# A hybrid attention layer on one core: k and q interleaved by channel in DRAM, and a later product with the softmax reciprocals

## The chip, the cores and the metric

The kernel runs on one core of one Trainium2 chip. The time is the device time of one execution in microseconds; lower is better. A core has five engines that run their own instruction streams and wait for each other by semaphores: TensorE (PE, with its weight loads PEld), VectorE (DVE), ScalarE (ACT), GpSimd (POOL) and SyncE (SP). Here SP computes nothing: it issues nearly all the DMA transfers, one after the other. POOL issues a few.

## The reference

One post-norm residual layer on x of 512 positions by 2048 channels, all in float32. One projection by w_in gives eight blocks of 1024 columns: q, k, v and a gate for each of two head groups, 16 heads of 64 channels each.

```python
h = einsum(x, w_in); qa, ka, va, ga, qb, kb, vb, gb = split(h)
# group A: three dilated windows, merged with weights proportional to their denominators, T5 bias
ya = dilated_attention(qa, ka, va, t5_bias)
# group B: windows of 8 rows x 16 columns on the 8 x 64 grid of positions, learned 2-D bias
yb = neighbourhood_attention(qb, kb, vb, na_rpb)
y  = concat(ya * silu(ga), yb * silu(gb))
x  = layer_norm(alpha * x + y @ w_out)
```

Everything goes through softmax(q k / 8 + bias) v per head, with masks that differ by group.

## The kernel before

**Numbers in two parts.** Float32 operands of TensorE are split into a high part (rounded to the matmul type) and a low part (the rest). A product takes three matmuls: high x high, high x low, low x high. ScalarE makes the high part (a copy), VectorE the low part (a subtraction). In the names, `wh` and `wl` are the two parts of weights, `th` and `tl` of the turned probabilities, `yk` of the gated output.

**Stages.** First the projections: a plain block of gate columns, then the blocks k, q, v of group 0, k of group 1, a block of gates, q and v of group 1, each a seven-product Strassen scheme (`strassen_block`, run by `run_blocks`). A block of 28 jobs loads its weights in 16 tiles of 512 KB (`braw`). Their results are turned, split and stored to DRAM by `store_kq` and `store_v`. Then attention: 16 pairs of heads, groups in turn, each head in four query blocks, so 128 steps of scores and some more for what follows them. Into its steps filler matmuls are mixed (`fill`): the remaining gate units and half of the output projection. Then the other half of the output projection and the layer norm.

**The q and k tiles.** `store_kq` holds for two heads of a pair a tile `kst`: 128 partitions (64 channels of head a = 0, then of a = 1), high and low. A k tile goes to `k_d[pair]` as [high/low, channel, head, position]; in SBUF the load puts high rows on partitions 0 to 63 and low rows on 64 to 127. A q tile goes to `q_d[pair]` as [high/low, 128 rows of head and channel, position], in rows of 64 positions (256 bytes). `load_kq` reads for a pair one k tile and three q tiles: high on both halves of `qt`, low on the lower half of `ql`. The upper half of `ql` is zeroed once for each of two buffers. Scores are then two matmuls: `qt` with k (high x high + high x low), `ql` with k (low x high).

**Steps of attention.** Step n works on pair i = n // 8. In it stand the scores of block n, the reduction on VectorE that adds the bias and takes the minimum (L623, `s` and `mn`), the exponential on ScalarE (L627, `p`), and the turning of the probabilities of step n - 2 on TensorE (`pt`, L686) with their split (L691, L692). At steps with n % 4 = 2 TensorE multiplies the turned probabilities of a head by v (`pv`, L708); the two halves are added on ScalarE (L832) and VectorE (L833) into `y`. `pv` takes one of the two "sc" buffers in PSUM that the scores use.

**Normalisation.** A pair's eight denominators are inverted at n % 8 = 0 (L844), turned at n % 8 = 1 by `share`, sent to DRAM and read back broadcast into `rc` by POOL (L722, L724). `gate` multiplies `y` by the gate at n % 8 = 4 (L731). `gated` then queues three operations: y times rc on VectorE (L739), the high part on ScalarE a step later (L740), the low part on VectorE two steps later (L741). Here `gated` of pair i - 1 is called at n % 8 = 7 of pair i.

**What sets the order.** On PE, DVE and ACT the projections and attention stand as the program is written (a manual schedule); in attention SP's order is written too. During the projections SP's and POOL's orders come from a scheduler that works on a timeline of its own. `later(k, ...)` puts an operation at the end of the k-th step from now; an operation for VectorE that falls on a step with n % 4 = 1 is held until after the next step's reduction.

Of the kernel before, what the change touches and what calls it, by code (L numbers as in the profile page):

```python
# [6 lines left out]
F32 = mybir.dt.float32  # L7
# [6 lines left out]
S = 512  # L14
H = 16
KT = D // 128
PAIRS = 8
# [42 lines left out]
def _view(t, offset, dims):  # L60
    return bass.AP(tensor=t.tensor, offset=t.offset + offset, ap=dims)
# [10 lines left out]
def hybrid_layer(tc, xT, xn, w_in, w_early, w_mid, w_gate, w_out, t5x, brow, rpb, cmask, eye, gain, lbias, out):  # L72
    nc = tc.nc
    from contextlib import ExitStack
    with ExitStack() as ctx:
# [8 lines left out]
        def f(ap):  # L84
            return ap.bitcast(F32)
# [44 lines left out]

        rows_d = dram.tile([H, 16, ROW], F32, name="rows_d")
        bias_d = dram.tile([H, 128, 560], F32, name="biasa_d"), dram.tile([H, 128, BW], F32, name="biasb_d")
        k_d = [dram.tile([PAIRS, 2, 64, 2, S], F32, name=f"k{g}_d") for g in range(2)]
        q_d = [dram.tile([PAIRS, 2, 128, S], F32, name=f"q{g}_d") for g in range(2)]
        sg_d = dram.tile([2 * PAIRS, 128, S], F32, name="sg_d")
        rc_d = dram.tile([2 * PAIRS, 8, 128], F32, name="rc_d")
        v_d = [dram.tile([PAIRS, 128, 4, 256], F32, name=f"v{g}_d") for g in range(2)]
# [92 lines left out]
        def store_kq(kind, g, ch, half, b, src):  # L230

            o = vst.next("kst", F32R)
            hi, lo = o[:, 0:512], o[:, 512:1024]
            if kind == "k":
                split(src, hi, lo)
            else:
                nc.scalar.activation(hi, src, AF.Copy, scale=-0.125)
                nc.vector.scalar_tensor_tensor(lo, src, -0.125, f(hi), op0=ALU.mult, op1=ALU.subtract)
            o = o.rearrange("p (s n q) -> p s n q", s=2, n=2)
            for n in range(2):  # L240
                for i in range(2):
                    if kind == "k":
                        to = k_d[g][4 * ch + 2 * b + n].rearrange("s c a q -> c s a q")[:, :, i]
                        nc.sync.dma_start(to[:, :, HALF * half:HALF * half + HALF], f(o[64 * i:64 * i + 64, :, n]))
                    else:
                        to = q_d[g][4 * ch + 2 * b + n][i].rearrange("c (b h q) -> c h b q", b=4, h=2)[:, half]
                        nc.sync.dma_start(to, f(o[:, i, n].rearrange("p (b q) -> p b q", b=4)))

        def turned_out(kind, two, b):

# [323 lines left out]
        lows = []  # L574
        for i in range(2):
            ql = slot(f"t{4 * i + 3}", F32R, "ql").rearrange("p (a n) -> p a n", a=2)
            nc.gpsimd.memset(f(ql[64:128]), 0.0)
            lows.append(ql)

        def load_kq(i):  # L580

            g, j = ORDER[i]
            t0 = 4 * (i % 2)
            kt = slot(f"t{t0}", F32R, "k").rearrange("p (a n) -> p a n", a=2)
            qt = slot(f"t{t0 + 1}", F32R, "q").rearrange("p (a n) -> p a n", a=2)
            ql = lows[i % 2]

            nc.sync.dma_start(f(kt.rearrange("p a n -> p (a n)")), k_d[g][j].rearrange("s c a q -> (s c) (a q)"))
            for n, to in enumerate((qt[0:64], qt[64:128], ql[0:64])):
                nc.sync.dma_start(f(to), q_d[g][j][n // 2].rearrange("(a c) q -> c a q", a=2))  # L590
            loaded[i] = qt, ql, kt

        def load_v(i):
# [212 lines left out]
        with tc.manual_schedule(engines=engines):  # L806
# [6 lines left out]
            for n in range(136):  # L813
                b, i = n % 4, n // 8
                mixing = n % 4 == 2 and 6 <= n <= 130
                amount = ((8, 6, 1, 6) if n < 64 else (8, 7, 1, 7))[b]
                if b == 0 and n < 124:
                    load_bias(n // 4 + 1)
                if n % 8 == 0 and n < 120:
                    load_kq(i + 1)  # L820
                if n % 8 == 4 and n < 128:
                    if n < 120:
                        load_v(i + 1)
                    load_sg(i)
                exponent = scores(n) if n < 128 else None
                while held:
                    held.pop(0)()
                if mixing:
                    if exponent:
                        exponent()  # L830
                    mine, theirs, y, t = values(n // 4 - 1)
                    nc.scalar.activation(t, theirs, AF.Copy)  # L832
                    nc.vector.tensor_tensor(y, mine, t, ALU.add)  # L833
                    fill(amount)
                else:
                    fill(amount // 2)
                if 2 <= n < 130:
                    turn(n - 2)
                if not mixing:
                    if exponent:  # L840
                        exponent()
                    fill(amount - amount // 2)
                if n >= 8 and n % 8 == 0:
                    later(0, lambda i=i: nc.vector.reciprocal(dens[i - 1], dens[i - 1]), True)  # L844
                if n >= 8 and n % 8 == 1:
                    share(i - 1)
                if n >= 8 and n % 8 == 4:
                    later(0, lambda i=i: gate(i - 1), True)
                if n >= 8 and n % 8 == 7:
                    gated(i - 1)  # L850
                close()
            while tasks:
# [144 lines left out]
        for dc in (2, 3):  # L997
            for u in range(4, 8):
                raw = out_ring.next("wraw")
                nc.sync.dma_start(raw[:, :1024], w_out[8 * dc + u])  # L1000
                i = 2 * (u - 4)
# [92 lines left out]
```

## Time and profile before

| | |
|---|---|
| median of 3 runs | 974.61 us (974.07 to 975.96) |
| profiled execution | 975.21 us, span 973.4 us |
| granted TensorE clock | 0.999 |
| TensorE busy | 964.3 us (99%) |
| VectorE, ScalarE, POOL busy | 757.0, 496.3, 181.3 us |
| read from and written to HBM | 148.69 and 44.50 MB |

The span runs from the first to the last instruction. A row of instructions gives the engine, the line of the program, the operation, what it writes and reads, a count and the busy time; in brackets or behind a bar stands the idle time of that engine before it, and the instruction that ended it. In a timeline the first two numbers are the start and the length in microseconds, of several instructions where a count follows. "SPq" rows are issues: what they move lands later. A tile is named without its buffer's number.

### The profile page before, as it was taken

Reading aid. Unit: us, or ns where it says so; the run is one execution under the profiler, and the core shown is the slowest. Engines: PE = TensorE matmul, PEld = TensorE weight load, DVE = VectorE, ACT = ScalarE, POOL = GpSimd, SP = SyncE. Lnnn points to the kernel's source line nnn. Section 1 sums busy time; section 2 is a strip of 40 time slices with the busy share of each in tenths; the row PEclk is TensorE's granted clock in tenths of the full one; section 3 lists DMA queues with packets and bytes.
Section 4 is the critical chain, followed back from the end, with each engine's and each line's share of the span. In section 5 each row is a group of like instructions: output and inputs, shape, how many; then the busy total and the mean of one; then the engine's idle time right before and its main releaser. Section 6 shows DMA issues by size and latency. Waiting matters only on the chain. (4 is left out here: it accounts for less than half of the span.)

```text
span 973.4 us, 13993 instructions
## 1 busy us (share of the span) xinstructions
PE 964.3 (99%) x4789; PEld 803.6 (83%) x4789; DVE 757.0 (78%) x1144; ACT 496.3 (51%) x857; POOL 181.3 (19%) x323
## 2 busy tenths in 40 slices
PE   8999999999999999999999999999999999999997
PEld 6887888888888889988888888888888888888886
DVE  7897778679789777796788856777776777777877
ACT  7454444444444344443445446776766766672300
POOL 1006656835636000000000000011111000100020
PEclk9999999999999999999999999999999999999999
DMA  9715796698396087420872687887887678779213
GB/s 336 277 65 133 229 329 210 171 296 235 107 350 207 33 282 206 163 93 17 266 182 103 206 271 209 224 234 212 236 239 218 204 228 204 209 219 314 91 58 117
DMA packets 120263, 194.18 MB, mean 199 GB/s; under 512 B 49455, under 2 KB 69807, under 8 KB 120192
## 3 DMA queue, kind: packets, MB, share of 16 engines
q1 hardware_dynamic: 107520, 169.68, 57.3%
q0 software_dynamic: 12096, 22.95, 8.5%
q8 instruction: 38, 0.62, 0.3%
q10 hardware_dynamic: 576, 0.66, 0.2%
q14 instruction: 33, 0.27, 0.1%
HBM read 148.69 MB, written 44.50 MB: 198 GB/s over the span
## 5 line engine op out<-in xcount | busy, mean ns | idle before, releaser
L376 ACT ACTIVATE wh<-braw 128x1024 fp32r<-128x1024 f32 x182 | 193.3, 1062 | 269.2 <-PE acc L404 206.5
L381 DVE TENSOR_TENSOR wl<-braw,wh 128x1024 fp32r<-128x1024 f32 x182 | 223.6, 1230 | 53.8 <-ACT wh L376 53.6
L403 PE MATMUL acc<-wh,xk 128*128 128x512 f32 x384 | 151.3, 394 | 0.0
L405 PE MATMUL acc<-wl,xk 128*128 128x512 f32 x384 | 149.7, 390 | 0.0
L404 PE MATMUL acc<-wh,xk 128*128 128x512 f32 x384 | 149.5, 389 | 0.0
L372 DVE TENSOR_TENSOR braw<-braw 128x1024 f32<-128x1024 f32 x104 | 126.6, 1217 | 0.1
L403 PE MATMUL acc<-wh,op 128*128 128x512 f32 x288 | 113.1, 393 | 0.0
L405 PE MATMUL acc<-wl,op 128*128 128x512 f32 x288 | 112.2, 390 | 0.0
L404 PE MATMUL acc<-wh,op 128*128 128x512 f32 x288 | 112.1, 389 | 0.0
L756 PE MATMUL acc<-wh,yk 128*128 128x512 f32 x320 | 108.1, 401 | 0.0
L692 DVE TENSOR_TENSOR tl<-pt,th 128x256 fp32r<-128x256 f32 (+1 forms) x128 | 71.0, 555 | 35.8 <-ACT th L691 34.1
L691 ACT ACTIVATE th<-pt 128x256 fp32r<-128x256 f32 (+1 forms) x128 | 62.3, 489 | 47.6 <-PE pt L686 45.4
L403 PEld LDWEIGHTS acc<-wh,xk 128*128 128x128 f32 x384 | 72.1, 188 | 15.3 <-ACT bias L151 0.9
L405 PEld LDWEIGHTS acc<-wl,xk 128*128 128x128 f32 x384 | 72.1, 188 | 15.2
L404 PEld LDWEIGHTS acc<-wh,xk 128*128 128x128 f32 x384 | 72.2, 188 | 14.5
L627 ACT ACTIVATE p<-s,mn 128x512 f32<-128x512 f32 (+1 forms) x96 | 62.2, 648 | 29.4 <-DVE mn L623 29.0
L623 DVE CUSTOM_DVE_ANT_0 s<-sc,biases 128x512 f32<-128x512 f32 (+2 forms) x128 | 67.7, 529 | 10.8 <-PE sc L667 10.0
L562 PE MATMUL acc<-xk,wh 128*128 128x512 f32 x256 | 75.3, 404 | 0.0
L756 PEld LDWEIGHTS acc<-wh,yk 128*128 128x128 f32 x320 | 58.5, 189 | 8.8
L161 POOL DMA_DIRECT2D bias<-rows_d x128 | 61.6, 489 | 17.6 <-DMA biasa_d<-bias 5.5
L756 PE MATMUL acc<-wl,yk 128*128 128x512 f32 x160 | 63.9, 403 | 0.0
L405 PEld LDWEIGHTS acc<-wl,op 128*128 128x128 f32 x288 | 54.1, 188 | 11.4
(188 smaller groups left out, 1708.2 us busy)
## 6 DMA issues: line engine op xcount, KB each, us to landing
braw<-in_w_in SPq DMA_DIRECT2D x96, 512.0 KB
wraw<-in_w_out SPq DMA_DIRECT2D x32, 512.0 KB
k_d<-kst SPq DMA_DIRECT2D x64, 128.0 KB
q_d<-kst SPq DMA_DIRECT2D x64, 128.0 KB
v_d<-vst SPq DMA_DIRECT2D x32, 256.0 KB
q<-q_d SPq DMA_DIRECT2D x32, 256.0 KB
wraw<-in_w_gate SPq DMA_DIRECT2D x16, 512.0 KB
k<-k_d SPq DMA_DIRECT2D x16, 512.0 KB
```

The source lines that it names most:

```text
L372: nc.vector.tensor_tensor(raws[q][u], raws[q][u], raws[other][u], ALU.add)
L376: nc.scalar.activation(h, raws[q][u], AF.Copy)
L381: nc.vector.tensor_tensor(l, raws[q][u], f(h), ALU.subtract)
L403: nc.tensor.matmul(accs[t], ah[:, q], h[:, c], start=first and k == 0, stop=False, skip_group_check=skip)
L404: nc.tensor.matmul(accs[t], al[:, q], h[:, c], start=False, stop=False, skip_group_check=skip)
L405: nc.tensor.matmul(accs[t], ah[:, q], l[:, c], start=False, stop=k == 7, skip_group_check=skip)
L562: nc.tensor.matmul(acc, w[:, k * 128:k * 128 + 128], X[8 * u + k][:, s], start=u == 0 and n == 0 and k == 0, stop=u == 1 and n == 2 and k ...
L623: nc.vector.tensor_tensor_reduce(*flat, bias, 1.0, 3e38, ALU.add, ALU.min, mn)
L627: nc.scalar.activation(p[:, to:to + n].rearrange("p (b r c) -> p b r c", r=8, c=c), s[:, :n].rearrange(order, r=8, c=c), AF.Exp, bias=mn, ...
L691: nc.scalar.activation(th, pt[:, :nch], AF.Copy)
L692: nc.vector.tensor_tensor(tl, pt[:, :nch], f(th), ALU.subtract)
L756: nc.tensor.matmul(acc[:, part], yk[k][:, s, c], w[:, wk], start=first and kk == 0 and n == 0, stop=last and kk == 1 and n == 2)
```

## The change

The k tile is stored and loaded as [channel, high/low, head, position], so that partition 2c holds the high row of channel c and 2c + 1 its low row. The q tile is stored as [high/low, channel, head, position]; a channel's two heads now stand side by side, so a row to load has 4096 bytes. Since the two heads lie on different partitions of `kst`, a store of q is cut in two, one a head. `qt` is loaded by one transfer that reads each row twice (a step of 0), `ql` by one that fills the even partitions; the odd ones are zero, and the zeroing covers the whole tile. `gated(i - 2)` is called at n % 8 = 1 for pairs 0 to 13; the last two pairs keep their steps.

```diff
-        k_d = [dram.tile([PAIRS, 2, 64, 2, S], F32, name=f"k{g}_d") for g in range(2)]
-        q_d = [dram.tile([PAIRS, 2, 128, S], F32, name=f"q{g}_d") for g in range(2)]
+        k_d = [dram.tile([PAIRS, 64, 2, 2, S], F32, name=f"k{g}_d") for g in range(2)]
+        q_d = [dram.tile([PAIRS, 2, 64, 2, S], F32, name=f"q{g}_d") for g in range(2)]
...
-                        to = k_d[g][4 * ch + 2 * b + n].rearrange("s c a q -> c s a q")[:, :, i]
+                        to = k_d[g][4 * ch + 2 * b + n][:, :, i]
                         nc.sync.dma_start(to[:, :, HALF * half:HALF * half + HALF], f(o[64 * i:64 * i + 64, :, n]))
                     else:
-                        to = q_d[g][4 * ch + 2 * b + n][i].rearrange("c (b h q) -> c h b q", b=4, h=2)[:, half]
-                        nc.sync.dma_start(to, f(o[:, i, n].rearrange("p (b q) -> p b q", b=4)))
+                        to = q_d[g][4 * ch + 2 * b + n][i].rearrange("c a (b h q) -> c a h b q", b=4, h=2)[:, :, half]
+                        for a in range(2):
+                            nc.sync.dma_start(to[:, a], f(o[64 * a:64 * a + 64, i, n].rearrange("p (b q) -> p b q", b=4)))
...
-            nc.gpsimd.memset(f(ql[64:128]), 0.0)
+            nc.gpsimd.memset(f(ql), 0.0)
...
-            nc.sync.dma_start(f(kt.rearrange("p a n -> p (a n)")), k_d[g][j].rearrange("s c a q -> (s c) (a q)"))
-            for n, to in enumerate((qt[0:64], qt[64:128], ql[0:64])):
-                nc.sync.dma_start(f(to), q_d[g][j][n // 2].rearrange("(a c) q -> c a q", a=2))
+            nc.sync.dma_start(f(kt.rearrange("p a n -> p (a n)")), k_d[g][j].rearrange("c s a q -> (c s) (a q)"))
+            nc.sync.dma_start(f(qt.rearrange("p a n -> p (a n)")), _view(q_d[g], j * 256 * S, [[2 * S, 64], [0, 2], [1, 2 * S]]))
+            nc.sync.dma_start(f(ql[0:128:2].rearrange("p a n -> p (a n)")), q_d[g][j][1].rearrange("c a q -> c (a q)"))
...
-                if n >= 8 and n % 8 == 7:
+                if n % 8 == 1 and 2 <= i < 2 * PAIRS:
+                    gated(i - 2)
+                if n % 8 == 7 and i >= 2 * PAIRS - 1:
                     gated(i - 1)
```

TensorE's order is the same. SP, from the stores of group 1's q to the end of the loads of x that follow (`q_d` the stores, `braw` the weights of the next block, `xback` the part of x that attention's fillers need again), before:

```order
L247 DMA q_d<-kst 512x1x64 x4
L360 DMA braw<-in_w_in 128x1024
L247 DMA q_d<-kst 512x1x64 x4
L360 DMA braw<-in_w_in 128x1024 x7
L247 DMA q_d<-kst 512x1x64 x4
L360 DMA braw<-in_w_in 128x1024
L247 DMA q_d<-kst 512x1x64 x4
L360 DMA braw<-in_w_in 128x1024
L247 DMA q_d<-kst 512x1x64 x16
L522 DMA xback<-in_xT 128x256 x5
L360 DMA braw<-in_w_in 128x1024
L522 DMA xback<-in_xT 128x256 x3
```

and now:

```order
L248 DMA q_d<-kst 64x4x64 x16
L361 DMA braw<-in_w_in 128x1024 x2
L248 DMA q_d<-kst 64x4x64 x8
L361 DMA braw<-in_w_in 128x1024 x4
L248 DMA q_d<-kst 64x4x64 x8
L361 DMA braw<-in_w_in 128x1024 x4
L248 DMA q_d<-kst 64x4x64 x32
L361 DMA braw<-in_w_in 128x1024 x3
L523 DMA xback<-in_xT 128x256
L361 DMA braw<-in_w_in 128x1024
L523 DMA xback<-in_xT 128x256 x7
```

There are 64 stores for 32, the weight loads stand behind more of them, and seven of the eight loads of x have moved behind four weight loads. On VectorE the splits of that x (`xk<-xback`) have moved with them, in the new order:

```order
L373 TENSOR_TENSOR braw<-braw 128x1024
L89 TENSOR_TENSOR xk_98<-xback,xk_98 128x256
L382 TENSOR_TENSOR wl<-braw,wh 128x1024
L89 TENSOR_TENSOR xk_99<-xback,xk_99 128x256
L89 TENSOR_TENSOR xk_100<-xback,xk_100 128x256
L89 TENSOR_TENSOR xk_101<-xback,xk_101 128x256
L89 TENSOR_TENSOR xk_102<-xback,xk_102 128x256
L89 TENSOR_TENSOR xk_103<-xback,xk_103 128x256
L89 TENSOR_TENSOR xk_104<-xback,xk_104 128x256
L382 TENSOR_TENSOR wl<-braw,wh 128x1024
L89 TENSOR_TENSOR xk_105<-xback,xk_105 128x256
L382 TENSOR_TENSOR wl<-braw,wh 128x1024 x2
```

Before, they stood one or two at a time between the `wl` and `braw` operations of five earlier jobs; now six stand in one piece. In attention, VectorE of pair 2 from step 18 to step 21 (`ISA` is the reduction of the scores, `y<-y,rc` the product with the reciprocals, `yk` the low part), before:

```order
L741 SCALAR_TENSOR_TENSOR yk<-y,yk 128x512
L833 TENSOR_TENSOR y<-pv,tmp 64x512
L692 TENSOR_TENSOR tl<-pt,th 128x4x128
L568 SCALAR_TENSOR_TENSOR sgo<-sgo,acc 128x512
L623 ISA s,mn<-sc,biases 128x512
L623 ISA mn 128x1
L692 TENSOR_TENSOR tl<-pt,th 128x4x128
L548 TENSOR_TENSOR wl<-wraw,wh 128x1024
L623 ISA s,mn<-sc,biases 128x512
L623 ISA mn 128x1
L692 TENSOR_TENSOR tl<-pt,th 128x4x128
L731 TENSOR_TENSOR y<-y,sg 128x512
```

and now:

```order
L740 TENSOR_TENSOR y<-y,rc 128x512
L834 TENSOR_TENSOR y<-pv,tmp 64x512
L693 TENSOR_TENSOR tl<-pt,th 128x4x128
L569 SCALAR_TENSOR_TENSOR sgo<-sgo,acc 128x512
L624 ISA s,mn<-sc,biases 128x512
L624 ISA mn 128x1
L693 TENSOR_TENSOR tl<-pt,th 128x4x128
L549 TENSOR_TENSOR wl<-wraw,wh 128x1024
L742 SCALAR_TENSOR_TENSOR yk<-y,yk 128x512
L624 ISA s,mn<-sc,biases 128x512
L624 ISA mn 128x1
L693 TENSOR_TENSOR tl<-pt,th 128x4x128
```

The product has taken the low part's place at step 18, and the low part stands at the end of step 19, behind `wl`. At step 15, where the product stood behind another `wl`, nothing has come in its stead.

## The prediction

> **What bounds the kernel now.** I read the page's first two parts first, then the busy time by stage, then what the weight loads of TensorE waited for. Weight loads (PEld) are read instead of matmuls, because a matmul's modelled end hides short gaps.
>
> ```profile
> span 973.4 us, 13993 instructions
> PE 964.3 (99%) x4789; PEld 803.6 (83%) x4789; DVE 757.0 (78%) x1144; ACT 496.3 (51%) x857; POOL 181.3 (19%) x323
> ```
>
> The execution with this span took 975.21 us, 1.8 us more than its span. TensorE is busy 99%, so only its idle moments can be won back, and anything else must first become late for it. Attention, where the loads and the normalisation lie, runs from about 575 to 880 us. Its row of the table by stage (in order: length, TensorE, weight loads, VectorE, ScalarE, POOL, then the granted clock, 1.00), and what the weight loads waited for in it (total, times, longest):
>
> ```profile
> 575.00:880.00 305.00, 304.61 (x1651) 253.19 (x1651) 223.57 (x523) 208.53 (x494) 28.61 (x54) 1.00 0.79 222
> ...
> PEld pv L708 <- ACT th L691: 1.5, 4, 0.4
> PEld pt L717 <- issue: 0.4, 2, 0.2
> PEld pv L708 <- issue: 0.3, 1, 0.3
> PEld pv L708 <- DVE mn L623: 0.2, 1, 0.2
> ```
>
> The four rows add up to 2.4 us: that is all that attention can return. No DMA is among them, so no q, k or v load is waited for. The chain of waits nevertheless ends far back at the copy of the reciprocals, which the change gives two more steps:
>
> ```profile
> 680.11 5.90 DMA rc<-rc_d
> ```
>
> A place on that chain is no price: it is paid only where a row of the four above stands.
>
> **Part 1: the q stores.** Each store of a (pair, high or low) tile becomes two of 64 channels, 64 more issues on SP's queue, in two projection blocks (q of group 0 and of group 1). What an issue holds SP:
>
> ```profile
> L247 SPq DMA_DIRECT2D q_d<-kst x64: 512/637/3278, 188.9 to 506.3; - x64
> L244 SPq DMA_DIRECT2D k_d<-kst x64: 574/599/1179, 109.6 to 387.3; - x64
> ```
>
> The k store is already a 64-partition store and takes 599 ns, the whole q store 637: issuing seems to cost per store, not per byte. So I take 0.65 us a half store (pace of the row 465.34 below: 2.61/4), with bounds 0.33 (half of it) and 0.70. 64 more are 42 us of SP time, 21 in each block. Group 1's block is the harder, as it ends with eight loads of x (xback). SP today:
>
> ```profile
> 465.34 2.61 SPq L247 DMA_DIRECT2D q_d<-kst  x4
> ...
> 471.50 6.06 SPq L360 DMA_DIRECT2D braw<-in_w_in  x7
> 477.65 5.94 SPq L247 DMA_DIRECT2D q_d<-kst  x4
> 483.68 2.81 SPq L360 DMA_DIRECT2D braw<-in_w_in  x1
> ...
> 507.02 2.48 SPq L522 DMA_DIRECT2D xback<-in_xT  x5
> 509.60 0.38 SPq L360 DMA_DIRECT2D braw<-in_w_in  x1
> ...
> 511.49 4.61 SPq L360 DMA_DIRECT2D braw<-in_w_in  x3
> ```
>
> With the ten weight loads that the order above shows among the 32 stores, now 64 x 0.65 + 10 x 0.4 = 46 us follow 465.3: the last store ends at 511 instead of 507. Then come four weight loads, the last of which cannot start before 515.8 (511.49 + 4.61 - 0.33, its buffer), and seven loads of x at 2.48/5 = 0.5 each: the last is issued at about 519.5 instead of 511.5. What waits for it stands on VectorE:
>
> ```profile
> 524.49 0.41 DVE L89 TENSOR_TENSOR xk<-xback,xk 128x256 fp32r<-128x256 f32 x1
> 525.41 1.23 DVE L381 TENSOR_TENSOR wl<-braw,wh 128x1024 fp32r<-128x1024 f32 x1 [0.50 <-ACT wh L376]
> 528.12 1.23 DVE L381 TENSOR_TENSOR wl<-braw,wh 128x1024 fp32r<-128x1024 f32 x1 [1.49 <-ACT wh L376]
> 530.79 1.23 DVE L381 TENSOR_TENSOR wl<-braw,wh 128x1024 fp32r<-128x1024 f32 x1 [1.45 <-ACT wh L376]
> ```
>
> In the new order six of the x splits stand just before the wl of 525.41. SP's landings are not recorded; the nearest recorded one is a POOL copy, median 2.7 us:
>
> ```profile
> bias<-rows_d POOLq DMA_DIRECT2D x128, 35.0 KB, 2.7
> ```
>
> 519.5 + 2.7 = 522.2, then about 0.4 us each on ScalarE and VectorE: 523, within the place. Past it VectorE has 0.50 + 1.49 + 1.45 = 3.4 us of idle time before anything is late for TensorE. So I book **0**; the cover is those 3.4 us and some 2 before them, and with it gone each microsecond of SP's lateness costs one. The other end is rival C. Weight loads pushed behind the stores move by 5 to 10 us and are also booked at 0, with the same cover spent first.
>
> By the Trainium skill ("DMA: Bandwidth & Descriptors", Rules for kernel authors) a transfer should not be split into two disjoint partition halves: the halves share the same engines and gain nothing. By that rule the 42 us buy no transfer time and are a loss wherever SP is not covered; the sum stays, its weight lies on rival C. No run here shows yet whether a half moves faster.
>
> **Part 2: the q loads.** Three loads of 2048-byte rows become two of 4096:
>
> ```profile
> L590 SPq DMA_DIRECT2D q<-q_d x32: 579/600/988, 537.3 to 835.0; - x32
> L590 SPq DMA_DIRECT2D ql<-q_d x16: 598/605/1117, 541.8 to 835.6; - x16
> ```
>
> SP spends 1.8 us a pair on them now, and 0.6 + 0.4 to 0.6 after (the duplicated one as before, the plain one between the 0.38 of the plain load at 509.60 and 0.6). Since TensorE waits for no load, a saving of at most 0.8 us a pair is worth **0**; bytes stay the same. The zeroing of ql takes all 128 partitions instead of 64:
>
> ```profile
> 540.66 0.95 POOL L577 MEMSET ql<- 64x1024 f32 x1 [221.63 <-PE acc L404]
> 578.56 0.59 POOL L569 DMA_DIRECT2D sg_d<-sgo  x1 [28.02 <-DVE sgo L568]
> ```
>
> At worst it doubles to 1.9 us, and POOL has 28 us of idle time behind it: **0**. The k layout changes addresses alone: as many rows of the same 1024 bytes, **0**.
>
> **Part 3: y times the reciprocals.** The product (VectorE, 0.69 in the row below), the copy (ScalarE, 0.62) and the low part (VectorE, as long as the product: both read 128x512) go two steps later. What the first of the four stalls looks like, ScalarE, VectorE and the weight loads around step 18:
>
> ```profile
> 614.56 0.72 ACT L627 ACTIVATE p<-s,mn 128x512 f32<-128x512 f32 x1 [1.68 <-DVE mn L623]
> ...
> 615.29 0.62 ACT L740 ACTIVATE yk<-y 128x512 fp32r<-128x512 f32 x1
> 615.81 0.36 ACT L691 ACTIVATE th<-pt 128x256 fp32r<-128x256 f32 x1
> ...
> 611.39 1.22 DVE L548 TENSOR_TENSOR wl<-wraw,wh 128x1024 fp32r<-128x1024 f32 x1
> 613.23 0.69 DVE L739 TENSOR_TENSOR y<-y,rc 128x512 f32<-128x512 f32 x1 [0.62 <-DMA rc<-rc_d]
> ...
> 616.22 0.42 PEld L708 LDWEIGHTS pv<-th,vv 128*128 128x128 f32 x3 [0.39 <-ACT th L691]
> ```
>
> The value product pv waits 0.39 us for th. Ahead of th on ScalarE stand the exponential, late because VectorE was held by wl, the wait for rc and y times rc, and then the copy yk. Both moved operations leave this place: 0.69 (VectorE) and 0.62 (ScalarE) are freed, more than the longest wait of 0.4. All four go: **-1.5** (bounds -1.5 and 0).
>
> They arrive elsewhere. The product takes the place that the low part had, a swap of like for like. The low part now stands a step on, before the other pv of the pair (step 22 for pair 2), where VectorE looks like this:
>
> ```profile
> 622.00 1.22 DVE L548 TENSOR_TENSOR wl<-wraw,wh 128x1024 fp32r<-128x1024 f32 x1
> ...
> 624.34 0.68 DVE L731 TENSOR_TENSOR y<-y,sg 128x512 f32<-128x512 f32 x1
> 624.94 0.68 DVE L623 CUSTOM_DVE_ANT_0 s<-sc,biases 128x512 f32<-128x512 f32 x1
> ...
> 625.70 0.76 PEld L708 LDWEIGHTS pv<-th,vv 128*128 128x128 f32 x4 [0.34 <-issue]
> ```
>
> No bracket stands before these VectorE rows: it does not idle here, and pv already waits 0.34 us, until the scores' reduction of 624.94 is done (there are two "sc" banks, and pv takes the one that it frees). One more operation ahead costs its pace, 624.94 - 624.34 = 0.60. The new order puts wl and the low part side by side in pairs 2, 6, 13, 14 and 15, so this can cost from 0 to 5 x 0.6 = 3.0. The last three come where a step has more filler matmuls (7 for 6 from step 64 on), so I charge 0.5 in pairs 2 and 6 and next to nothing later: **+1.1**.
>
> **Sum.** 0 + 0 - 1.5 + 1.1 = -0.4 us. Of the profiled 975.21 that makes 974.8; this execution lies 0.6 above the median of the three runs, 974.61, so the forecast is 974.61 - 0.4 = **974.2 us**. Runs of this kernel spread from 974.07 to 975.96; about 0.2% (1.9 us) is what a measurement can tell from no change.
>
> **Rivals.** *A, the forecast*: one set of short waits is traded for another; 973.2 to 976.5.
>
> *B, all of attention's waits go*: the low part fits because VectorE is idle 27% of the stage (223.57 of 305). Against it: no idle time at the very place. Price: up to -2.4, so 972.2 to 973.0.
>
> *C, SP becomes late*: for it, SP's rows above hold excess that I left out: 6.06 - 7 x 0.4, 5.94 - 2.61 and 2.81 - 0.4, together 9.0 us in which an issue was held up. If it comes on top, the last load of x is issued at 528, lands at 531 and passes the 5 us of cover by about 3; 0.70 for a half store adds 3 more. Against: halves are issued slower than the whole stores filled the queue. It decides from an issue at about 524.5 on. Price 2 to 5 us: 976.5 to 979.5, around 977.5.
>
> *D, the low part stalls all five places*: -1.5 + 3.0 = +1.5, so 976.1. Against: the larger steps later.
>
> **How the numbers follow.** A 0.70, B 0.08, C 0.17, D 0.05. Faster by over 0.2% (below 972.7) takes the better half of B and little else: 0.05. Slower by over 0.2% (above 976.6) is nearly all of C and the top of A and D: 0.19. The rest, 0.76, is no change. The range 973.2 to 977.2 holds A and D and the near end of C, and leaves out most of B and the far half of C.
>
> **What would show it.** The waits of PEld in attention: pv on th falls from 1.5 to below 0.3, and pv on VectorE's reduction (or on nothing shown) rises from 0.5 to over 1, at steps 22 and 54. VectorE no longer waits for rc. SP: 64 more q issues near 0.6 us, the last load of x issued before 524, and no new wait of TensorE between 185 and 575 us. A wait of acc on wl at 526 to 535 us means C. I am wrong if a TensorE wait over 2 us appears anywhere, or if attention gains over 2.

## The result

The changed kernel took a median of 980.38 us (978.52 to 984.49, 6 runs); the kernel before, run beside it, took 974.21 us (973.51 to 975.96, 6 runs). The ratio is 1.0065, with a 95% interval of 1.0043 to 1.0087: slower, by about 6 us. The forecast was 974.2 us, no change. Run again in a later session (below, "the whole change once more"), it took 979.46 us, ratio 1.0049 (1.0036 to 1.0061).

The page of the profiled execution after the change begins:

```profile
span 978.2 us, 14044 instructions
PE 966.1 (99%) x4789; PEld 803.8 (82%) x4789; DVE 757.9 (77%) x1144; ACT 496.4 (51%) x857; POOL 189.7 (19%) x323
```

TensorE still reads 99%. At this size of difference the busy share says nothing; the waits do. What the weight loads waited for after the change (in total, times, longest; rows that stand much alike before are left out):

```profile
PEld acc L406 <- DVE wl L382: 2.6, 3, 1.3
...
PEld pv L709 <- ACT th L692: 1.6, 2, 0.8
PEld acc L404 <- ACT wh L377: 1.4, 1, 1.4
...
PEld pv L709 <- issue: 0.4, 1, 0.4
...
PEld acc L757 <- DVE yk L742: 0.3, 1, 0.3
PEld pt L718 <- issue: 0.2, 1, 0.2
```

The first and third rows, 4.0 us together, are new, and they are in the projections. The attention rows add up to 2.5 us, for 2.4 before.

**Where the time went.** TensorE runs the same 4789 matmuls in the same order in all the kernels of this table, so the start of one matmul in one trace can be set against its start in another. The table gives, for each stage, what a kernel's profiled execution lost (+) or won (-) against the profiled execution of before: the change of that difference over the stage. Nothing over 0.05 us arises between 260 and 515 us except in one of these runs, told of below, and nothing after 885 us.

| kernel | 0 to 185 us | q of group 0, to 260 | q and v of group 1, 515 to 575 | attention, to 885 | median us | ratio (95%) |
|---|---|---|---|---|---|---|
| whole change | -0.3 | +1.2 | +3.9 | 0.0 | 980.38 | 1.0065 (1.0043 to 1.0087) |
| whole change once more | -0.2 | +1.1 | +3.7 | +0.1 | 979.46 | 1.0049 (1.0036 to 1.0061) |
| layout and loads, product at its old step | +0.2 | +0.8 | +5.3 | -1.0 | 978.93 | 1.0038 (1.0023 to 1.0052) |
| split stores alone | -0.7 | +1.0 | +3.0 | +0.3 | 978.41 | 1.0037 (1.0023 to 1.0050) |
| later product alone | -0.2 | 0.0 | 0.0 | 0.0 | 974.82 | 0.9993 (0.9983 to 1.0003) |
| change without split | -0.7 | 0.0 | 0.0 | 0.0 | 974.64 | 1.0000 (0.9991 to 1.0009) |
| second halves issued by POOL | -0.9 | 0.0 | 0.0 | 0.0 | 974.84 | 0.9999 (0.9990 to 1.0008) |
| x loads issued by POOL | -1.1 | +1.9 | 0.0 | +0.1 | 976.43 | 1.0018 (1.0008 to 1.0028) |

The first column is the start of the program. It is below zero in all but one row: the profiled execution of before, 975.21 us, lost up to 1.1 us more there than the others, which is part of its distance from the median. The stages of the whole change add up to 4.8 us. The ratios are each against runs of before in the same session, whose medians were 974.2 to 975.2 us. The split of the q stores stands behind all of it.

**SP in group 1's q block, after** (timeline: start, length, count):

```profile
466.22 11.19 SPq L248 DMA_DIRECT2D q_d<-kst  x16
...
494.95 23.54 SPq L248 DMA_DIRECT2D q_d<-kst  x32
518.59 1.50 SPq L361 DMA_DIRECT2D braw<-in_w_in  x3
520.19 0.38 SPq L523 DMA_DIRECT2D xback<-in_xT  x1
520.66 0.54 SPq L361 DMA_DIRECT2D braw<-in_w_in  x1
521.25 4.88 SPq L523 DMA_DIRECT2D xback<-in_xT  x7
```

The last store ends at 518.5 (before 507), and the loads of x are issued between 520.2 and 526.1 (before 507.0 to 511.4). ScalarE, which makes the high parts of x and of the weights, in the order in which they are queued:

```profile
519.75 1.06 ACT L377 ACTIVATE wh<-braw 128x1024 fp32r<-128x1024 f32 x1 [1.66 <-PE acc L405]
525.68 0.42 ACT L88 ACTIVATE xk<-xback 128x256 fp32r<-128x256 f32 x1 [4.86 <-DMA xback<-in_xT]
526.00 1.04 ACT L377 ACTIVATE wh<-braw 128x1024 fp32r<-128x1024 f32 x1
528.81 2.12 ACT L88 ACTIVATE xk<-xback 128x256 fp32r<-128x256 f32 x6 [1.77 <-DMA xback<-in_xT]
530.84 1.04 ACT L377 ACTIVATE wh<-braw 128x1024 fp32r<-128x1024 f32 x1
```

The first load of x, issued at 520.19, has landed only at 525.6, and ScalarE stood 4.86 us before it, with the next `wh` queued behind. Then come the six splits that the new order has in one piece, and the next `wh` behind these. The six went at the pace of their own loads: by the semaphore updates in the trace (a transfer counts one up as its parts land) the second load had landed at 528.8 and the seventh, issued at 525.3, at 530.5. TensorE pays 0.27 us for the first load and the two longer waits for these six, seen at its weight loads:

```profile
528.36 0.19 PEld L406 LDWEIGHTS acc<-wl,op 128*128 128x128 f32 x1 [0.27 <-DVE wl L382]
...
531.93 0.19 PEld L404 LDWEIGHTS acc<-wh,op 128*128 128x128 f32 x1 [1.41 <-ACT wh L377]
532.04 0.19 PEld L405 LDWEIGHTS acc<-wh,op 128*128 128x128 f32 x1
533.19 0.19 PEld L406 LDWEIGHTS acc<-wl,op 128*128 128x128 f32 x1 [0.96 <-DVE wl L382]
```

**Group 0's q block, after**, all engines on one timeline:

```profile
230.28 0.60 ACT L237 ACTIVATE kst<-pt 128x512 fp32r<-128x512 f32 x1 [3.38 <-DMA q_d<-kst]
...
232.78 0.19 PEld L406 LDWEIGHTS acc<-wl,op 128*128 128x128 f32 x1 [1.34 <-DVE wl L382]
```

Here it is not a load that is late. The store buffers `kst` come free when the stores out of them have landed; ScalarE waits 3.38 us for a buffer, and the weights queued behind it are late for TensorE by 1.3 us. Before, ScalarE has no such wait there. How much of the late landing is the late issue, and how much the four weight loads that the new order issues in one piece ahead of these stores, is not shown.

**Attention, after.** VectorE and, below, the weight loads at step 22 of pair 2:

```profile
626.27 1.22 DVE L549 TENSOR_TENSOR wl<-wraw,wh 128x1024 fp32r<-128x1024 f32 x1
627.40 0.68 DVE L742 SCALAR_TENSOR_TENSOR yk<-y,yk 128x512 fp32r<-128x512 f32 x1
628.01 0.68 DVE L624 CUSTOM_DVE_ANT_0 s<-sc,biases 128x512 f32<-128x512 f32 x1
```

```profile
630.58 0.76 PEld L709 LDWEIGHTS pv<-th,vv 128*128 128x128 f32 x4 [0.79 <-ACT th L692]
```

The low part sits behind `wl`, the reductions move by 0.6 us, and pv waits 0.79 us for 0.34 before. The same happens at step 54. The four old waits are gone.

### The profile page after: what moved, and what is told of

The parts are those of the page before. It is cut to its first block, busy times and chain, and to the rows that moved or that the text cites. A ratio compares the mean times of both kernels' runs of the same rounds, so it can differ in the third digit from the quotient of the medians.

```text
span 978.2 us, 14044 instructions
## 1 busy us (share of the span) xinstructions
PE 966.1 (99%) x4789; PEld 803.8 (82%) x4789; DVE 757.9 (77%) x1144; ACT 496.4 (51%) x857; POOL 189.7 (19%) x323
## 4 chain that ended last, share of the span: by engine, by line
PE 93%; DMA 4%; DVE 2%; ACT 1%; issue 0%; SPq 0%; DVEq 0%; ACTq 0%
PE acc L757 16%; PE acc L406 14%; PE acc L404 14%; PE acc L405 14%; PE acc L563 9%; PE pv L709 5%; PE pt L687 4%; PE sc L668 2%; PE sc L667 2%; DMA braw<-in_w_in 2%; PE acc L280 1%; PE sc L757 1%; PE acc L281 1%; PE acc L282 1%; PE acc L395 1%; PE acc L396 1%
## 5 line engine op out<-in xcount | busy, mean ns | idle before, releaser
L404 PEld LDWEIGHTS acc<-wh,op 128*128 128x128 f32 x288 | 54.4, 189 | 12.3 <-ACT wh L377 1.4
```

Of the source, the lines that this page charges most:

```text
L404: nc.tensor.matmul(accs[t], ah[:, q], h[:, c], start=first and k == 0, stop=False, skip_group_check=skip)
```

## The experiments

**1. The change without its third part** (layout, stores and loads of the change, `gated` at its old step).

```diff
-                if n % 8 == 1 and 2 <= i < 2 * PAIRS:
-                    gated(i - 2)
-                if n % 8 == 7 and i >= 2 * PAIRS - 1:
+                if n >= 8 and n % 8 == 7:
                     gated(i - 1)
```

> The change without its third part: k and q interleaved, stores split, two loads, but the product with the reciprocals at its old step. Theory (the loss is SP's lateness by the split stores, and attention's gain and cost cancel): 979 to 983 us, within 1 us of the whole change, with TensorE waits of some 4 us in all at about 527 to 534 us and 1 us near 232 us, and the four old waits of pv for th (1.5 us in all) back. Rival (the later product costs what was lost): within 1 us of before, 973.5 to 975.5.

Measured: 978.93 us, ratio 1.0038 (1.0023 to 1.0052). The waits of the weight loads:

```profile
PEld acc L406 <- DVE wl L382: 2.9, 3, 1.0
PEld acc L404 <- ACT wh L377: 2.3, 2, 1.4
...
PEld pv L709 <- ACT th L692: 0.7, 2, 0.4
```

The loss in the projections stays without the later product. It is 1.4 us less than the whole change in its first session and 0.5 less than in its second, with intervals that overlap. One detail was missed: only two of the four old waits for `th` came back. Why is told under "what was not expected".

**2. The third part alone** (old layout, stores and loads; `gated` as in the change).

> The third part alone: old layout, old stores and loads, the product two steps later. Theory: 973.8 to 974.8 us, no difference that can be measured; waits of pv for th fall from 1.5 us to at most 0.3, and TensorE loses about 0.5 us each at steps 22 and 54 instead. Rival (the later product is what costs): 978 us or more. Rival (it is a gain that the stores hide): 973.0 or less.

Measured: 974.82 us, ratio 0.9993 (0.9983 to 1.0003): no difference. The longest of attention's waits of the weight loads:

```profile
PEld pv L708 <- ACT th L691: 1.6, 2, 0.8
```

Against before the same matmuls gain 0.31, 0.41, 0.39 and 0.33 us at the four old places, the matmul behind each wait counted in (1.4 in all). They lose 0.45 us at step 22, 0.64 at step 54, 0.2 at step 118 (pair 14), and 0.13 where a matmul of the output projection waits for the low part itself (1.4). So the sizes at steps 22 and 54 came as expected, but the name did not: the two new waits are listed under `th`, not under the reduction, and the total under `th` stays where it was. This execution also has 1.5 us on top around 300 us, where ScalarE waited for a `vst` buffer whose store had not landed; the change does not touch that place.

**3. The split stores alone** (old layout, loads and product).

```diff
-                        nc.sync.dma_start(to, f(o[:, i, n].rearrange("p (b q) -> p b q", b=4)))
+                        for a in range(2):
+                            nc.sync.dma_start(to[64 * a:64 * a + 64], f(o[64 * a:64 * a + 64, i, n].rearrange("p (b q) -> p b q", b=4)))
```

> Only the q stores are split into two of 64 partitions; layout, loads and the step of the product are those of before. Theory (number of issues on SP): 979 to 983 us, last load of xback issued at about 525 us instead of 511, waits of TensorE at 527 to 534 us. Rival (the interleaved addresses or the loads with 4096-byte rows make the loss): 973.5 to 975.5 us. In between if both have a part.

Measured: 978.41 us, ratio 1.0037 (1.0023 to 1.0050). The stores' row (shortest, median and longest issue in ns) and the new waits:

```profile
L248 SPq DMA_DIRECT2D q_d<-kst x128: 507/613/1718, 188.3 to 518.1; - x128
```

```profile
PEld acc L406 <- DVE wl L382: 3.1, 3, 1.2
PEld acc L404 <- ACT wh L377: 1.6, 2, 1.4
```

A median 0.6 us under the expected range, but the same places and nearly the same waits as the whole change: neither the interleaved addresses nor the long rows are needed for the loss.

**4. One store for the interleaved layout.** A channel's row in DRAM is ordered block, head, position, so that one store of three dimensions reaches it.

```diff
-                        to = q_d[g][4 * ch + 2 * b + n][i].rearrange("c a (b h q) -> c a h b q", b=4, h=2)[:, :, half]
-                        for a in range(2):
-                            nc.sync.dma_start(to[:, a], f(o[64 * a:64 * a + 64, i, n].rearrange("p (b q) -> p b q", b=4)))
+                        at = (4 * ch + 2 * b + n) * 256 * S + i * 128 * S + HALF // 4 * half
+                        nc.sync.dma_start(_view(q_d[g], at, [[128, 2], [256, 256], [1, 64]]), f(o[:, i, n]))
...
-            nc.tensor.matmul(o, qt[:, a, cols], ko, start=True, stop=False)
+            nc.tensor.matmul(o, qt[:, b, a], ko, start=True, stop=False)
...
```

> The whole change, but a q tile is stored by one transfer again: a channel's row in DRAM is ordered block, head, position, so that channel and block have one step, and the scores pick their 128 columns from that order. Loads stay two with 4096-byte rows, k stays interleaved, the product stays two steps later. Theory: 973.8 to 974.8 us, SP's order and times of the q block as before (last load of xback issued by 513 us), no wait at 527 to 534 us; the new loads and the new layout alone are worth nothing. Rival (layout or loads make the loss): 978 us or more. Rival (the loads are a gain that the split stores hide): 973.0 or less.

Measured: 1143.54 us, ratio 1.1725 (1.1709 to 1.1741), and no theory had it. The stores' row:

```profile
L247 SPq DMA_DIRECT2D q_d<-kst x64: 491/3561/11502, 188.9 to 673.7; - x64
```

A store held SP for a median of 3.56 us instead of 0.64, and longest for 11.5. All the loss is in the two q blocks and what follows them (+86.8 us to 260 us, +48.7 to 515, +33.3 to 575, nothing in attention), so the run says nothing against the loads; it only adds a new fault of its own, the outermost dimension of two. By the Trainium skill ("DMA: Bandwidth & Descriptors", "Why a DMA increments its semaphore by 16 and not by 1") a transfer is spread over the largest number of engines up to 16 that divides the outermost dimension on both sides, which would be two here. The trace agrees: its semaphore shows three updates for a store of this run, one at the issue and two landings, and 16 for a store of before. Each of the two engines then carries eight times as much, and the row agrees with a much slower store. The shortest issue, 0.49 us, is no longer than before's: the stores right behind another one were held. The question of this experiment went to the next ones.

**5. The loads of x issued by POOL**, which is idle there.

```diff
-            nc.sync.dma_start(back[:, k], xT[2 * k][:, HALF:])
+            nc.gpsimd.dma_start(back[:, k], xT[2 * k][:, HALF:])
```

> The whole change, but POOL (idle from 400 to 540 us) issues the eight loads of xback instead of SP; the q stores stay split on SP. Theory (the split stores make the x loads late, and these hold ScalarE and VectorE): the waits of TensorE at 526 to 534 us fall from 3.9 us to below 1, the 1.2 us near 232 us stays: 975.5 to 977. Rival (the weights behind the stores are late as well): waits of 2 us or more stay there, 978 or more.

Measured: 976.43 us, ratio 1.0018 (1.0008 to 1.0028). POOL issued the loads at 506.64 us, while SP was as late as in the whole change:

```profile
506.64 4.44 POOL L523 DMA_DIRECT2D xback<-in_xT  x8 [186.96 <-PE acc L406]
```

```profile
510.06 9.27 SPq L248 DMA_DIRECT2D q_d<-kst  x14
519.42 1.97 SPq L361 DMA_DIRECT2D braw<-in_w_in  x4
```

The whole 3.9 us at 526 to 537 us went; the weights behind the stores, as late as before, held nobody. What stays is group 0's wait (1.9 us in this execution). So in group 1 it is the late loads of x alone. This run does not tell how much of their lateness is SP's count of issues and how much the weights that stood ahead of them in its queue.

**6. The second half stores issued by POOL.**

```diff
-                            nc.sync.dma_start(to[:, a], f(o[64 * a:64 * a + 64, i, n].rearrange("p (b q) -> p b q", b=4)))
+                            (nc.gpsimd if a else nc.sync).dma_start(to[:, a], f(o[64 * a:64 * a + 64, i, n].rearrange("p (b q) -> p b q", b=4)))
```

> The whole change, but the second half store of each q tile is issued by POOL: 64 q issues on SP as before, as many half stores in all as after. Theory (number of issues on SP): last load of xback issued before 516 us, no wait at 526 to 534 us, 973.8 to 975.5 us. Rival (half stores move their bytes slower, whoever issues them): waits there stay, 977.5 or more.

Measured: 974.84 us, ratio 0.9999 (0.9990 to 1.0008).

```profile
L248 SPq DMA_DIRECT2D q_d<-kst x64: 574/599/1312, 188.0 to 505.5; - x64
L248 POOL DMA_DIRECT2D q_d<-kst x64: 631/632/661, 188.3 to 507.5; - x64
```

128 half stores, the long rows, the interleaving and the later product are all there, and both losses are gone. Only SP's count of issues went back, and with it SP's order to nearly that of before. A rule bears on this: by the Trainium skill ("DMA: Bandwidth & Descriptors", Rules for kernel authors) spreading transfers over issuing engines saves issue time alone, not transfer time. The rows agree: the loss went when 64 issues left SP. The half stores of POOL also travel in a queue of their own, which this run does not separate; run 7, with all 128 on SP's queue, does so for group 1.

**7. Stores cut in two another way**: 128 partitions each, half of the blocks of positions; all else as before.

```diff
-                        nc.sync.dma_start(to, f(o[:, i, n].rearrange("p (b q) -> p b q", b=4)))
+                        for c in range(0, 4, 2):
+                            nc.sync.dma_start(to[:, c:c + 2], f(o[:, i, n].rearrange("p (b q) -> p b q", b=4)[:, c:c + 2]))
```

> Kernel before, each q store cut in two another way: 128 partitions each, half of the blocks of positions. Theory (an issue costs the same 0.6 us whatever it carries): as the split by partitions, 977 to 981 us, pace of the stores 0.65 us. Rival (it is the 64 partitions that are slow): 973.8 to 975.5 us.

Measured: 977.27 us, ratio 1.0023 (1.0014 to 1.0032): at the lower edge of the theory's range, and by luck. The profiled execution lost 0.9 us in group 0, nothing in group 1's block, and 1.4 us in attention, which this edit does not touch.

```profile
L248 SPq DMA_DIRECT2D q_d<-kst x128: 359/467/1961, 188.7 to 511.7; - x128
```

```profile
517.00 0.43 SPq L523 DMA_DIRECT2D xback<-in_xT  x1
```

As many issues of as many bytes, but one costs 0.47 us, not 0.61: the theory's equal price per issue was wrong. The last load of x goes out at 517.0, and no wait appears at 526 to 537 us. This gives the place of the step: an SP that is done with x at 517 is in time, one that starts with it at 520 is not. The order differs too: here the first four loads of x stand behind one weight load, in the change the first stands behind three.

**8. The change without its split**: q in DRAM as before and stored whole; k interleaved, q loaded into interleaved partitions (three loads of 2048-byte rows), the whole of `ql` zeroed, the product two steps later.

```diff
...
-            nc.sync.dma_start(f(qt.rearrange("p a n -> p (a n)")), _view(q_d[g], j * 256 * S, [[2 * S, 64], [0, 2], [1, 2 * S]]))
+            for a in range(2):
+                nc.sync.dma_start(f(qt[:, a]), _view(q_d[g], (4 * j + a) * 64 * S, [[S, 64], [0, 2], [1, S]]))
...
```

> The change without its split: q in DRAM as before and one store a tile; k interleaved, q loaded into interleaved partitions (high part by one load a head that reads each 2048-byte row twice, low part into the even partitions, three loads as before), the whole tile ql zeroed, the product two steps later. Theory: 973.8 to 974.9 us, SP's q block as before, no wait at 526 to 534 us; attention as with the later product alone. Rival (interleaving itself costs): 977 or more.

Measured: 974.64 us, ratio 1.0000 (0.9991 to 1.0009). Interleaving, zeroing and the later product cost nothing together, and with run 6 beside it (two loads of 4096-byte rows, 974.84 us) the long rows bring nothing either.

**9. The product four steps later.**

```diff
-                if n >= 8 and n % 8 == 7:
+                if n % 8 == 3 and 2 <= i < 2 * PAIRS and i != 9:
+                    gated(i - 2)
+                if n % 8 == 7 and (i == 8 or i >= 2 * PAIRS - 1):
                     gated(i - 1)
```

> Kernel before with the third part put elsewhere: the product of a pair is queued four steps later than before (at step 3 of the pair after next), except for pair 7, whose result the output projection needs and which keeps its step. Its place is the least crowded on VectorE: no weight split stands between it and a pv. Theory: the four waits of pv for th (1.5 us) go, step 22 loses at most 0.2 us more than before and step 54 at most 0.1: attention gains 1.0 to 1.4 us, 973.0 to 974.2 us, near the limit of what can be told. Rival (the waits only move to other steps, as with two steps later): no gain in attention, 974.2 to 975.2.

Measured: 974.29 us, ratio 0.9997 (0.9988 to 1.0006); attention gained 0.6 us in the profiled execution. The expectation had its place wrong. At step 19 the product itself stands behind a weight split, and the wait at step 22 is as long as with the change:

```profile
620.74 1.22 DVE L548 TENSOR_TENSOR wl<-wraw,wh 128x1024 fp32r<-128x1024 f32 x1
621.88 0.68 DVE L739 TENSOR_TENSOR y<-y,rc 128x512 f32<-128x512 f32 x1
```

```profile
625.13 0.76 PEld L708 LDWEIGHTS pv<-th,vv 128*128 128x128 f32 x4 [0.82 <-ACT th L691]
```

**10. The whole change once more**, unedited.

> The whole change once more, unedited, beside the same runs of before as the others. Theory (attention's gain and cost cancel, so that the whole change costs what its split stores cost): 978 to 980 us, within 1 us of the change without its third part (978.9). Rival (the later product costs something more when the stores are split): 980.4 or more again.

Measured: 979.46 us, ratio 1.0049 (1.0036 to 1.0061): in the theory's range, and the interval overlaps that of run 1 (1.0023 to 1.0052).

**11. A place of its own for each pair.** As run 9, but pairs 0 and 4 have the product where the change has it, and their low part is queued four steps after it instead of two, away from the weight split of step 3.

```diff
-        def gated(i):
+        def gated(i, low=2):
...
-            later(2, lambda: nc.vector.scalar_tensor_tensor(t[:, 1], y, 0.5, f(t[:, 0]), op0=ALU.mult, op1=ALU.subtract), True)
+            later(low, lambda: nc.vector.scalar_tensor_tensor(t[:, 1], y, 0.5, f(t[:, 0]), op0=ALU.mult, op1=ALU.subtract), True)
...
-                if n >= 8 and n % 8 == 7:
+                if n % 8 == 1 and i in (2, 6):
+                    gated(i - 2, 4)
+                if n % 8 == 3 and 2 <= i < 2 * PAIRS and i not in (2, 6, 9):
+                    gated(i - 2)
+                if n % 8 == 7 and (i == 8 or i >= 2 * PAIRS - 1):
                     gated(i - 1)
```

> As the run with the product four steps later, but pairs 0 and 4 have the product where the whole change has it (step 2 of the pair after next), and their low part not behind the weight split of step 3 but held until after the reduction of step 6; pair 7 keeps its step. Theory (the wait at steps 22 and 54 comes from the operation that stands behind that weight split): no wait of pv over 0.4 us at any step, attention gains 1.0 to 1.5 us against before, 973.0 to 974.0 us. Rival (VectorE is full around step 22 whatever the order): the 0.45 us at step 22 stay, attention gains 0.6 or less.

Measured: 973.23 us (972.11 to 974.54, 11 runs), ratio 0.9983 (0.9975 to 0.9992): faster than both kernels, by about 1.7 us against before. All that the weight loads still waited for in attention:

```profile
PEld sc L666 <- DVE y L833: 0.5, 2, 0.3
PEld pv L708 <- issue: 0.4, 2, 0.2
PEld pt L717 <- issue: 0.2, 1, 0.2
```

The matmuls gain 1.2 us over attention. So VectorE was not full around steps 22 and 54; one operation of 0.6 us stood in the wrong place there.

**12. Only group 0's q stores split**, in the old layout.

```diff
-                        nc.sync.dma_start(to, f(o[:, i, n].rearrange("p (b q) -> p b q", b=4)))
+                        parts = (slice(0, 64), slice(64, 128)) if g == 0 else (slice(0, 128),)
+                        for p in parts:
+                            nc.sync.dma_start(to[p], f(o[p, i, n].rearrange("p (b q) -> p b q", b=4)))
```

> Kernel before with the q stores of group 0 alone split into two of 64 partitions, those of group 1 whole. Theory (each block loses by itself, group 0 through kst buffers whose stores land late): a wait of TensorE of 1 to 2 us near 232 us, none at 526 to 534 us, last load of xback issued by 512 us, 975.0 to 976.5 us. Rival (the lateness of the first block is what delays the second too): waits of 2 us or more at 526 to 534 us, 977.5 or more.

Measured: 976.37 us, ratio 1.0026 (1.0012 to 1.0040), in the theory's range. Group 1's block has no wait, as expected. But the profiled execution, 975.41 us and among the shortest of its runs, shows no wait of TensorE near 232 us either; ScalarE's wait for a buffer is there, shorter than the 3.38 us of the whole change:

```profile
228.59 0.60 ACT L237 ACTIVATE kst<-pt 128x512 fp32r<-128x512 f32 x1 [1.88 <-DMA q_d<-kst]
```

That 1.88 us can still be covered and 3.38 cannot fits the theory; that the other executions had the longer wait is not shown. This execution also lost 0.7 us in attention, which the edit does not touch, so the median is no clean price of group 0. That price is read from the traces of the kernels in which SP issues twice the stores in both groups: 0.8 to 1.9 us.

## Why the prediction was wrong

**The bound and the limit of the gain: right.** Only TensorE's waits counted, attention could return 2.4 us at most, and no kernel here got more than 1.2 us out of it.

**Part 1, the q stores: booked at 0, measured +5.1 us** (1.2 and 3.9 in the profiled execution). It is the step that failed, in four terms.

- *The issues.* 64 stores at 0.65 us and ten weights at 0.4 made 46 us after 465.3. The half store's price was right (0.61 us, with what lies between them 0.656). But the 64 stores took 46.7 us by the timeline (11.19 + 5.34 + 6.62 + 23.54), 5 us more than 64 x 0.65: issues were held up, as they were before. The prediction had seen that excess, 9.0 us, and left it to rival C. With the weights at 0.56 each and a start 0.9 us later, the last store ended at 518.5, not 511.
- *How late the loads of x are.* The last one was issued at 525.7, not 519.5, and had landed at 530.8, not 522.2. The place that I held it against, the weight split behind six splits of x on VectorE, was the right one: the seventh load landed at 530.5, 6 us behind the 524.5 of that place, more than the 3.4 us of idle time that was to cover it, and the waits of 1.41 and 0.96 us follow. The first load has a place of its own that I left out. On ScalarE its split came due at 520.8, right behind the `wh` of 519.75; the load went out at 520.19, and its late landing cost TensorE 0.27 us.
- *The landing.* 2.7 us was assumed, from a POOL copy; the first load took 5.5 (520.19 to 525.68) and the seventh 5.2. SP's landings were called not recorded, but the semaphore updates in the trace of before hold them: the five loads of x ahead of a weight load landed after 2.2 to 2.9 us, the three behind it after 4.5 to 4.9. Ahead of the first load now stood the last stores and three weights of 512 KB, and the 16 DMA engines were busy throughout (their share in the column before the last, over 1.0):

```profile
524.00:526.00 2.00, 2.00 (x10) 1.65 (x10) 0.00 (x0) 0.32 (x1) 0.00 (x0) 1.00 1.02 405
```

- *Group 0's block.* "Group 1's block is the harder" was true, but for group 0 nothing was worked out at all. The loss there is not at a late load: the buffers of the stores themselves come free late, and that cost 1.2 us.

Rival C had the mechanism, the place (526 to 535 us) and the price (2 to 5 us, at 3.9) right, and a chance of 0.17; its total of 976.5 to 979.5 us falls short of the first session's median by about what group 0 adds. The signs spoke for C as well: a last load of x behind 524, and waits of acc on `wl` from 528 to 533 us. None of the waits reached 2 us by itself.

**The rule on halves: the trace agrees.** A half store was no cheaper to issue to speak of (0.61 for 0.64 us). Nor did it move faster to speak of: by the trace's semaphore updates the last four stores of group 1 landed 2.2 us after their issue as halves, and 2.2 to 2.4 us whole. Run 6 shows that the loss goes with the issues.

**Part 2, the loads: right, 0.** Runs 6 and 8. The zeroing of all 128 partitions took 0.96 us, as long as that of 64, not up to 1.9.

**Part 3, the product: both terms right, two small costs left out.** -1.5 was booked for the four old waits, and they returned 1.4; +1.1 was charged for steps 22 and 54, and they cost 1.1. Not booked were 0.13 us where a matmul of the output projection waits for the low part, and step 118 was charged next to nothing and cost 0.2. With these the net is 0.0 for the -0.4 of the sum. The sign that was to show it was named wrongly: pv on `th` did not fall, since the new waits end with `th` too, which the late reduction delays.

## What to carry to other kernels

Where one engine issues all the transfers, count its issues before their bytes: a transfer that is cut in two costs another issue (0.47 to 0.61 us here), and the price is paid by whatever is queued behind it. Look at every place where an in-order engine meets one of these loads: here the first had a small price, and the six that stand in one piece before a weight split had the large one. Excess in a queue's timeline that is not understood (here 9 us of held issues) belongs in the sum when the change lengthens that very queue, not in a rival. An operation moved off one crowded step should be checked against the instruction that it will stand behind at the new one; run 9 put the product behind a weight split and gained 0.6 us in its trace; run 11 chose the places of two pairs' products and low parts by themselves and gained 1.2.

## What was not expected of the hardware

**TensorE at half clock after short waits.** In the profiled execution of the whole change the granted clock (last column but two) fell to half behind the waits at 530 to 533 us, none of them longer than 1.4 us:

```profile
534.00:536.00 2.00, 2.00 (x6) 1.56 (x5) 2.00 (x3) 0.08 (x1) 0.00 (x0) 0.50 0.00 0
536.00:538.00 2.00, 2.00 (x7) 1.58 (x7) 1.78 (x4) 1.06 (x1) 0.00 (x0) 0.67 0.00 0
```

Seven matmuls started 0.43 us apart instead of 0.23 (3 us in all), so about 1.4 of the 3.9 us are this and not the waits themselves. Run 1 shows it too (eight matmuls); run 10, whose waits there are no smaller, does not, nor does run 3. By the Trainium skill ("TensorE: Matmul & The Clock Gate", Part 1) the clock is halved after an idle window of about 3.4 us that runs freely; the measured waits are shorter than that. On the window the trace agrees: in both runs the half clock lasted 3.41 us and began 529.07 us, or 155 times 3.413, after the clock had first come to full speed. In the window just before, TensorE was idle for 1.50 us (run 1: 1.52); in the windows of these waits run 10 has 1.27 at most and run 3 1.01. So a window that is not idle throughout can be enough. But one of run 5, near 230 us, has 1.61 us of idle time and no half clock behind it, so what decides stays open; the ends of matmuls, from which the idle time is reckoned, are modelled. The half clock may also be why the changed kernel's runs spread over 6.0 us and those of before over 2.5: of its six runs the two with the highest mean clock, 0.998, took 978.5 and 979.1 us, and the one with the lowest, 0.994, 984.5.

**The old step's price differs from trace to trace.** With the product at its old step VectorE waited for the broadcast of the reciprocals 1.2 us in all before, 0 in run 1, 1.5 in run 3, 1.9 in run 12 and 2.6 in run 7, and against before attention went -1.0, +0.3, +0.7 and +1.4 us in these four. With the later product no such wait is listed and attention's difference stayed between -0.05 and +0.11 us in all seven traces that have the change's step. The kernels with the old step differ in their projections and have one trace each, so it is not shown whether one kernel's executions differ as much. The four waits that the prediction priced may be one draw of these.

**An issue's price depends on its shape.** On SP a store of 512 rows of 256 bytes took 0.64 us, of 256 rows by 64 partitions 0.61, of 256 rows by 128 partitions 0.47, each as a median. With an outermost dimension of two the median was 3.56 and the shortest 0.49, so that most of the 3.56 is time in which SP was held behind the stores before, and not the price of an issue.
